# A streaming row maximum on one core: a tail recut into 29 loads, the clearing moved to GpSimd, and SyncE's implied waits dropped

## The chip, the cores and the metric

The kernel runs on one core of a Trainium2 chip. The metric is the device time of one execution in microseconds (us), as the median of several runs. A profiled execution also has a span, from the first to the last instruction of the program; in all profiles here the timed figure of the profiled run is 1.83 to 1.85 us above its span.

## The reference

```python
def setup_inputs():
    return {"x": np.random.randn(8192, 8192).astype(np.float32)}

def reference(x):
    return np.linalg.norm(x, ord=np.inf, axis=1)   # per row: the largest absolute value
```

268 MB are read once, and 8192 numbers are written.

## The kernel before

Rows lie on 128 partitions, 64 to a partition. The first 48 rows of each partition come in 24 bulk loads of two rows (16384 columns); VectorE reduces each in one instruction. The other 16 rows are the tail: seven tiles, each cut into some loads (`TAIL`), and a last tile whose cuts shrink to the end (`LAST`), so that little is left to reduce when the last byte has landed.

```python
TAIL = [
    [9728, 6656], [5632, 10752], [9600, 6784], [9344, 7040],
    [6784, 6528, 3072], [4736, 3072, 4224, 4352],
    [3968, 2432, 3072, 2944, 1792, 2176],
]
LAST = (      # (row of the pair, columns)
    [(0, w) for w in (2176, 2048, 1664, 1664)]
    + [(1, w) for w in (1536, 1280, 1152, 1024, 896, 896, 768)]
    + [(0, 640), (1, 640)]
)
...
nc.vector.memset(part[:], 0.0)
...
for j, (b, w) in enumerate(LAST):
    final = left[b] == 0
    ...
    nc.sync.dma_start(out=t[:, to : to + w], in_=...)
    if final:      # also reads the row's partial maxima, which lie just behind
        absmax(r_tail[:, r : r + 1], t[:, to : slot[b] + parts_of[b]])
    else:
        done = absmax(t[:, k : k + 1], t[:, to : to + w])
    ...
    if j == len(LAST) - 4:      # the bulk result's store waits for this reduction
        ins = nc.scalar.dma_start(out=out_b, in_=r_bulk[:])
        after(ins, done, ...)
nc.sync.dma_start(out=out_t, in_=r_tail[:])
```

The two final reductions of `LAST` wait for two things, a landing and VectorE's own counter (for the partial maxima). In the trace one of the two is a stand-alone wait, an instruction of its own in front of the reduction in VectorE's stream; here it is the wait for the landing (for the first of the two it ends at 622.25, and the reduction starts at 622.48).

## Time and profile before

| | kernel before, profiled run |
|---|---|
| time, median of the 3 first runs | 627.47 us |
| time of the profiled run itself | 627.57 us |
| span | 625.73 us |
| last bulk landing | 466.67 |
| last landing of all | 623.02 |
| end of VectorE's last reduction | 624.02 |
| store of the tail result issued, landed | 624.05, 625.47 |

Times inside a profile count from the start of the span. A landing is the issue of a load plus its time to landing. "Pitch" will mean the time from one VectorE start to the next when they run without a gap.

### The profile page before, as it was taken

What the parts mean: (1) busy time and instruction counts of PE and PEld (TensorE: products, weight loads), DVE (VectorE), ACT (ScalarE), POOL (GpSimd) and SP (SyncE); (2) the same over time, 40 slices, a digit from 0 to 9 for tenths busy, and PEclk for the clock granted to TensorE, in tenths of its full rate; (3) what the DMA queues carried; (4) which work ended last, traced back from release to release, by engine and by line L of the source; (5) the groups of instructions that cost most, each with busy time, mean ns of one, the idle gap of its engine ahead of it and who ended that gap; (6) DMA issues with size and microseconds to landing.
All of it is one profiled execution on the core that took longest, in us unless ns stands there. A gap on an engine that the chain in (4) does not pass through costs nothing.

```text
span 625.7 us, 205 instructions
## 1 busy us (share of the span) xinstructions
DVE 552.9 (88%) x67; POOL 0.2 (0%) x4
## 2 busy tenths in 40 slices
DVE  0588988889988889888898888988889999999998
POOL 0000000000000000000000000000000000000000
DMA  9999999999999999999999999999999999999997
GB/s 402 469 402 452 419 452 419 448 423 436 436 419 452 411 461 402 469 402 469 402 469 402 461 411 452 419 448 423 444 413 421 444 425 431 436 425 430 424 422 315
DMA packets 9282, 268.49 MB, mean 429 GB/s; under 512 B 1856, under 2 KB 1856, under 8 KB 3392
## 3 DMA queue, kind: packets, MB, share of 16 engines
q1 hardware_dynamic: 8496, 268.45, 99.5%
q10 hardware_dynamic: 784, 0.02, 0.1%
q14 instruction: 2, 0.02, 0.0%
HBM read 268.44 MB, written 0.03 MB: 429 GB/s over the span
## 4 chain that ended last, share of the span: by engine, by line
DMA 67%; DVE 31%; issue 1%; another core or an unknown queue 0%; DVEq 0%; SPq 0%
DMA t<-in_x_dram 67%; DVE r_bulk L140 24%; DVE part L140 6%; DVE t L140 2%; DVEq L230 0%; DVE r_tail L140 0%; SPq L159 0%
## 5 line engine op out<-in xcount | busy, mean ns | idle before, releaser
L140 DVE TENSOR_REDUCE r_bulk<-t 128x2 f32<-128x16384 f32 x24 | 413.3, 17220 | 69.7 <-DMA t<-in_x_dram 69.7
L140 DVE TENSOR_REDUCE part<-t 128x1 f32<-128x8192 f32 (+20 forms) x28 | 121.5, 4410 | 0.3 <-DMA t<-in_x_dram 0.3
L140 DVE TENSOR_REDUCE t<-t 128x1 f32<-128x1664 f32 (+8 forms) x11 | 16.7, 1576 | 0.2 <-DMA t<-in_x_dram 0.2
L140 DVE TENSOR_REDUCE r_tail<-t 128x1 f32<-128x644 f32 (+1 forms) x2 | 1.5, 814 | 0.0
L137 DVE MEMSET part<- 128x56 f32 x1 | 0.1, 105 | 0.9 <-PEq L219 0.9
L140 DVE TENSOR_REDUCE r_tail<-part 128x14 f32<-128x56 f32 x1 | 0.2, 201 | 0.0
L219 POOL MEMSET const-bfloat16-1.0<- 128x1 bf16 x1 | 0.1, 101 | 0.0
L219 POOL MEMSET const-uint8-127<- 128x1 uint8 x1 | 0.1, 101 | 0.0
L219 POOL MEMSET const-float32-0.0<- 128x1 f32 x1 | 0.1, 98 | 0.2 <-issue 0.2
L219 POOL MEMSET const-float32-1.0<- 128x1 f32 x1 | 0.1, 98 | 0.0
## 6 DMA issues: line engine op xcount, KB each, us to landing
t<-in_x_dram SPq DMA_DIRECT2D x2, 3392.0 KB, 37.2
t<-in_x_dram SPq DMA_DIRECT2D x1, 5376.0 KB, 40.5
t<-in_x_dram SPq DMA_DIRECT2D x1, 4864.0 KB, 32.9
t<-in_x_dram SPq DMA_DIRECT2D x1, 4800.0 KB, 32.9
t<-in_x_dram SPq DMA_DIRECT2D x1, 4672.0 KB, 34.7
t<-in_x_dram SPq DMA_DIRECT2D x3, 1536.0 KB, 36.9
t<-in_x_dram SPq DMA_DIRECT2D x1, 3520.0 KB, 42.7
t<-in_x_dram SPq DMA_DIRECT2D x1, 3328.0 KB, 40.4
```

Of the source, the lines that this page charges most:

```text
L137: nc.vector.memset(part[:], 0.0)
L140: return nc.vector.reduce_max(out=o, in_=i, axis=X, apply_absolute_value=True)
L219: nc = _bacc.Bacc("TRN2", target_bir_lowering=False, num_devices=1)
```

## The change

Its intent: fewer loads and fewer reductions in the tail (29 and 36 instead of 34 and 42), coarser cuts at the end, one instruction less on VectorE, and no waits on SyncE that another wait implies.

```diff
 TAIL = [
+    [6272, 10112],
+    [10112, 6272],
     [9728, 6656],
-    [5632, 10752],
-    [9600, 6784],
     [9344, 7040],
-    [6784, 6528, 3072],
-    [4736, 3072, 4224, 4352],
-    [3968, 2432, 3072, 2944, 1792, 2176],
+    [6144, 6784, 3456],
+    [6144, 5504, 4736],
+    [4352, 3840, 2816, 2944, 2432],
 ]
 LAST = (
-    [(0, w) for w in (2176, 2048, 1664, 1664)]
-    + [(1, w) for w in (1536, 1280, 1152, 1024, 896, 896, 768)]
-    + [(0, 640), (1, 640)]
+    [(0, w) for w in (2432, 2432, 2176)]
+    + [(1, w) for w in (1920, 1664, 1152, 1408, 1152)]
+    + [(0, 1152), (1, 896)]
 )
+def drop_implied_waits(nc):
+    ...   # of a load's waits, drop each that VectorE's instruction, waited for as well, has itself waited for
-    nc.vector.memset(part[:], 0.0)
+    nc.gpsimd.memset(part[:], 0.0)
...
+    nc.at_finalize(drop_implied_waits)
```

More of the change, by code (lines that the diff above doesn't have):

```diff
@@ L2 @@
+import copy
 import logging
@@ L96, in finish_on_pool @@
     end.instructions = [i for i in insts if i.name not in moved] + [wait, clear]
+def drop_implied_waits(nc):
+    sp, dve = mybir.EngineType.SP, mybir.EngineType.DVE
+    body = nc.main_func.blocks[-2]
+    insts = list(body.instructions)
+    counter, seen, upto = None, {}, []
+    for i in insts:
+        if i.engine != dve or i.sync_info is None:
+            continue
+        for s in i.sync_info.on_wait:
+            assert s.sync_type == "semaphore" and s.wait_mode == "sem-ge-imm"
+            seen[s.id] = max(seen.get(s.id, 0), s.wait_value)
+        for s in i.sync_info.on_update:
+            assert s.update_mode in ("sem-inc", "sem-add-imm")
+            assert counter in (None, s.id)
+            counter = s.id
+            upto += [dict(seen)] * s.update_value
+    for n, i in enumerate(insts):
+        if i.engine != sp or type(i).__name__ != "InstDMACopy":
+            continue
+        waits = i.sync_info.on_wait
+        at = [s.wait_value for s in waits if s.id == counter]
+        if len(waits) > 1 and at:
+            known = upto[max(at) - 1]
+            keep = [
+                s
+                for s in waits
+                if s.id == counter or s.wait_value > known.get(s.id, 0)
+            ]
+            insts[n] = copy.replace(
+                i,
+                sync_info=mybir.SyncInfo(
+                    on_wait=keep, on_update=list(i.sync_info.on_update)
+                ),
+            )
+    body.instructions = insts
 @with_exitstack
```

## The prediction

> **What bounds the kernel now.** I read the page first, then the DMA view, the busy times by stretch, the chain of work, the groups by form and the timeline of the last microseconds. The page:
>
> ```profile
> DMA  9999999999999999999999999999999999999997
> DMA packets 9282, 268.49 MB, mean 429 GB/s; under 512 B 1856, under 2 KB 1856, under 8 KB 3392
> q1 hardware_dynamic: 8496, 268.45, 99.5%
> L140 DVE TENSOR_REDUCE r_bulk<-t 128x2 f32<-128x16384 f32 x24 | 413.3, 17220 | 69.7 <-DMA t<-in_x_dram 69.7
> ```
>
> The load queue keeps the 16 DMA engines busy in all 40 slices; VectorE waits for loads in the bulk. The stretches (us, VectorE busy and instructions, GpSimd, clock, DMA share, GB/s) say where the rate is lower:
>
> ```profile
> 41.00:466.60 425.60, 378.84 (x22) 0.00 (x0) 1.00 1.00 433
> 466.60:600.00 133.40, 132.98 (x27) 0.00 (x0) 1.00 1.00 430
> 600.00:622.00 22.00, 21.77 (x15) 0.00 (x0) 1.00 1.00 416
> ```
>
> The DMA share stays 1.00 while the rate falls from 433 to 416 GB/s as loads shrink: a load costs something beyond its bytes. VectorE is busy 99% of the tail too, so both engines matter there. The chain (start, duration, what) dates the last bulk landing at 466.67 and shows the end:
>
> ```profile
> 425.94 40.74 DMA t<-in_x_dram
> 466.67 0.02 issue
> ...
> 590.91 21.42 DMA t<-in_x_dram
> 612.33 0.02 issue
> 612.35 9.89 DVE t L140 x8
> 622.25 0.23 issue
> 622.48 0.59 DVE r_tail L140
> ```
>
> From 612.35 the end is held by eight back-to-back reductions, not by a load. The timeline, rows from two answers of it, gives VectorE's rhythm and the last microseconds:
>
> ```profile
> 483.83 51.82 DVE L140 TENSOR_REDUCE part<-t 128x1 f32<-128x8192 f32 x9
> ...
> 621.73 0.41 ACTq L200 DMA_DIRECT2D out_dram<-r_bulk  x1
> 622.48 1.55 DVE L140 TENSOR_REDUCE r_tail<-t 128x1 f32<-128x644 f32 x2
> 624.05 0.35 SPq L202 DMA_DIRECT2D out_dram<-r_tail  x1
> ```
>
> Last, one row of the groups by form, and two of the DMA view of short stretches (the last load; the bulk result's store):
>
> ```profile
> L140 DVE TENSOR_REDUCE r_tail<-t 128x1 f32<-128x647 f32 x1 | 0.8, 815 | 0.0
> ```
>
> ```profile
> t<-in_x_dram SPq DMA_DIRECT2D x1, 320.0 KB, 8.8
> ```
>
> ```profile
> q10 hardware_dynamic: 784, 0.02, 7.5%
> ```
>
> The last load is issued at 614.18 and lands 8.84 later, at 623.02. Its reduction runs until 622.48 + 1.55 = 624.02, the store is issued at 624.05, and the span ends at 625.73: 1.68 us of store and closing barrier, which I take as fixed. The timed 627.47 is 1.74 above the span.
>
> [...]from 466.67 to 623.02 are 156.35 us; eight tiles of 16384 columns (512 B each over 128 partitions) take 154.20 us at 435.2 GB/s; the other 2.15 us over 34 loads are 0.063 us a load.[...] the nine reductions from 483.83 hold 49152 columns, 51.20 us at 0.96 GHz, so 0.62 us is left over 9, or 0.06 each after taking off the last one's overlap[...]. A single duration is longer than its pitch, columns / 0.96 GHz + 142 ns (647: 815).
>
> **The change part by part.**
>
> *Fewer loads.* Tail and last tile go from 21 + 13 = 34 loads to 19 + 10 = 29. Five times 0.063 is 0.32 us of DMA time, on the path of the last landing: 623.02 becomes about 622.70.
>
> *Fewer reductions.* VectorE's pieces go from 28 + 1 + 11 + 2 = 42 to 25 + 1 + 8 + 2 = 36. Six pitches' fixed parts are 0.36 us, but only useful if no new waiting comes in between, since the columns stay the same. I stepped through both tails with two rules: landings follow at columns x 1.1765 ns + 0.063 us; a reduction starts at the later of its landing + 0.03 and the last start + pitch. Before, the idle time sums to 0.83 us; after, to 1.28, as 6144, 4352 and 2432 columns are coarser to wait for. That takes 0.45 and more than eats the 0.36.
>
> *A wider end.* The last loads are 1408, 1152, 1152 and 896 where they were 896, 768, 640 and 640. Backwards from 622.70, an 896 load takes 1.117 us and a 1152 load 1.418, so the landings are 618.75, 620.17, 621.58, 622.70. The 1408 reduction starts at 618.78; pitch 1.527 puts the next at 620.31; pitch 1.260 would allow 621.57, its landing says 621.61; pitch 1.264 (1155 columns with the three partial maxima) puts the last at 622.88, 0.18 after its landing. It reads 901 elements: 0.939 + 0.142 = 1.080 us, where the 647 took 0.815. End: 623.96 against a measured 624.02. But the same stepping on the kernel before ends at 623.86, 0.16 short of the trace (the pipe's last loads do not land on a smooth line); if that error stays, the new end is 624.12. So the sum is between -0.06 and +0.10; I take +0.02.
>
> *The clearing on GpSimd.* VectorE's 0.1 us clearing lies at 0.87, long before the first landing at 21.97; nothing is gained. GpSimd's own runs after the opening barrier, equally hidden. It adds one semaphore to the closing waits. Built, these are five pairs where four were, and four of them fit before the store's landing: 0 to 0.05 us.
>
> *Implied waits.* SyncE's waits on a load that VectorE has consumed already end with the VectorE wait. Bulk loads are issued 40 us before they land and the queue never runs dry, so 0.
>
> *Smaller partial tile.* 42 values instead of 56 save [...]0.015 us, in the middle.
>
> *The bulk result's store.* It is still tied to the fourth reduction from the end, but that one now ends 3.6 us before the end of VectorE instead of 2.3. It took 7.5% of 5 us on each engine, 0.375 us. Before, it began after the last load's bytes. After, it is issued about 620.4 and its packets meet the last two loads.[...] With 0.18 us slack before the last reduction that is 0 to +0.2; I take +0.03.
>
> Sum: +0.02 + 0.01 + 0.03 = +0.06, so 627.5 us.
>
> **Rivals.** (1) *Landings alone set the end.* If VectorE really reaches the last load without a backlog, it ends at 622.70 + 0.03 + 1.08 = 623.81: -0.21, so 627.26. For it: six fewer reductions. Against: the chain shows eight reductions in a row without a gap. (2) *The store takes a full turn among the last loads.* The last landing moves to 623.07, VectorE ends at 624.18: +0.16, and with the 0.16 of the stepping +0.3, so 627.8. For it: its earlier issue.[...] (3) *The waits matter*, each costing SyncE time that holds back loads. It would show as DMA share under 1.00 in the bulk; that reads 1.00, so I give it almost nothing. (4) *Per-load cost is more than 0.063* where packets are small, since 416 GB/s rules at the end: 5 x 0.1 = 0.5 us off the landing, but the wider last reduction still stands, so 627.1 at best.
>
> **Range and chances.** The rivals span 627.1 to 627.8; another chip or day may add 0.1. I give 627.05 to 627.9. Faster by over 2% would need 614.9 us, under the 616.8 that the bytes alone take at 435.2 GB/s: 0.003. Slower by 2% needs 12.5 us of new stall in a queue that is 40 us ahead: 0.007. Within 2%: 0.99.
>
> **What would show each step right or wrong.** Last landing near 622.7; end of VectorE near 624.0; last reduction 1.08 us and starting about 0.2 after its landing; 433 GB/s unchanged in the bulk; store of the bulk result issued near 620.4 to 620.6, its packets among the last loads. Wrong would be: a last landing later than 623.0 (the store or the loads' cost), a gap before the last reduction (rival 1), a DMA share under 1 in the tail, or a bulk that moves at all.

Passages that no trace or run of this case shows are cut from it, and the cuts are marked. The numbers that stay can be read from the profile of the kernel before. A straight line through the tail's 34 steps from one landing to the next, against their columns, gives 1.1766 ns a column and 0.063 us a load; with 512 bytes a column that is 435.2 GB/s. (Without the one step that took 0.44 us longer, see below, it gives 1.1795 ns and 0.040 us, so the split hangs on that load.) No load of this profile took less than 1.1767 ns a column, which is what the 616.8 us for all bytes rests on. The 0.96 GHz stands for VectorE's columns: of the gapless reductions one of 8192 columns starts 8.593 us before the next and one of 896 columns 0.993 us, which is 1.042 ns a column, or 0.96 columns a ns, and 0.06 us fixed. The 0.015 us of the smaller partial tile is 14 columns at that rate. The 0.1 us for another chip or day was a guess; the kernel before's medians lie between 627.47 and 627.74 us in all rounds.

The forecast's sum came to +0.06 us: 0.02 for the loads, reductions and wider end, 0.01 for the clearing and the partial tile, 0.03 for the bulk result's store. Of the last term the estimate inside the bracket is cut (0.06 us, from how the store's packets and the loads' would share the DMA engines). What remains of it is the bracket, 0 to 0.2 us: the store's measured 0.375 us (the "full turn" of rival 2) less the 0.18 us of slack. The 0.03 is the pick from it; without it the sum is +0.03, and 627.47 still becomes 627.5.

## The result

The changed kernel took 627.82 us (median of 6 runs, 627.73 to 628.22), the kernel before 627.53 us in the same rounds (6 runs, 627.43 to 627.70). A ratio is always the mean time of one kernel's runs over the mean of the other's in the same rounds, so it is not quite the ratio of the medians: here 1.0006, with a 95% interval of 0.9993 to 1.0019. By the 2% rule it is the same, and the interval cannot tell it from no change. The median is 0.32 us above the predicted 627.5, of which 0.06 is the kernel before having moved from 627.47 to 627.53.

Times of this size must be read inside the profile. The same three stretches of the changed kernel:

```profile
41.00:466.60 425.60, 378.84 (x22) 0.00 (x0) 1.00 1.00 432
466.60:600.00 133.40, 132.16 (x24) 0.00 (x0) 1.00 1.00 431
600.00:622.00 22.00, 21.96 (x12) 0.00 (x0) 1.00 1.01 421
```

The bulk moves at the same rate, and the last stretch is faster: 421 GB/s against 416. The loads did gain. The chain of work that ended last:

```profile
606.26 2.69 DVE t L180
608.95 0.10 DVE r_tail L180
...
609.07 12.92 DVE t L180 x7
622.00 0.32 issue
622.31 0.68 DVE r_tail L180
```

The piece from 609.07 is VectorE without a gap, as before. Then come 0.32 us under "issue", time in which the engine waited for nothing that the profile shows. The timeline of the end:

```profile
619.12 2.87 DVE L180 TENSOR_REDUCE t<-t 128x1 f32<-128x1408 f32 x2
620.76 0.42 ACTq L240 DMA_DIRECT2D out_dram<-r_bulk  x1
622.31 2.35 DVE L180 TENSOR_REDUCE r_tail<-t 128x1 f32<-128x1155 f32 x2 [0.33 <-DVE t L180]
624.70 0.35 SPq L242 DMA_DIRECT2D out_dram<-r_tail  x1
```

And from the groups by form and the DMA view, the last reduction and the two last loads (issued at 606.18 and 611.65):

```profile
L180 DVE TENSOR_REDUCE r_tail<-t 128x1 f32<-128x901 f32 x1 | 1.1, 1082 | 0.0
```

```profile
t<-in_x_dram SPq DMA_DIRECT2D x1, 576.0 KB, 15.6
```

```profile
t<-in_x_dram SPq DMA_DIRECT2D x1, 448.0 KB, 11.3
```

The last load but one landed at 621.81, the last at 622.95. The reduction in front (1152 columns) started at 620.64, so its pitch of 1.26 us would have let the 1155 reduction start at 621.90. It started at 622.31, 0.41 us late by pitch and 0.50 after its data. The 0.33 in the bracket is the same hole counted from the end of the reduction in front, 621.98. The bracket names a VectorE instruction because VectorE's counter rose last before it; but the counter's value that the 1155 reduction waits for belongs to the third partial maximum of its row, whose reduction ended at 614.1. So the wait for the counter is not the cause.

One more line of the DMA view, for 622.9 to 623.4:

```profile
q14 instruction: 1, 0.01, 4.4%
```

This is one packet of 8192 bytes of kind instruction, as the profile names it, on queue q14, at 622.98, 0.67 us after the late start. The kernel before has such packets at 591.92 and 609.98, among the loads.

### The profile page after: what moved, and what is told of

Read it like the earlier page. It is cut to its first block, busy times and chain, and to the rows that moved or that the text cites. A ratio compares the mean times of both kernels' runs of the same rounds, so it can differ in the third digit from the quotient of the medians.

```text
span 626.4 us, 166 instructions
## 1 busy us (share of the span) xinstructions
DVE 552.5 (88%) x60; POOL 0.3 (0%) x5
## 4 chain that ended last, share of the span: by engine, by line
DMA 58%; DVE 40%; issue 2%; another core or an unknown queue 0%; DVEq 0%
DMA t<-in_x_dram 58%; DVE r_bulk L180 23%; DVE part L180 14%; DVE t L180 2%; DVEq L271 0%; DVE r_tail L180 0%
## 5 line engine op out<-in xcount | busy, mean ns | idle before, releaser
L180 DVE TENSOR_REDUCE part<-t 128x1 f32<-128x8192 f32 (+15 forms) x25 | 121.3, 4923 | 0.7 <-DMA t<-in_x_dram 0.7
L180 DVE TENSOR_REDUCE t<-t 128x1 f32<-128x2432 f32 (+5 forms) x8 | 15.6, 2011 | 0.0
L180 DVE TENSOR_REDUCE r_tail<-t 128x1 f32<-128x1155 f32 (+1 forms) x2 | 2.4, 1218 | 0.3 <-DVE t L180 0.3
```

What stands on the lines that cost most here:

```text
L180: return nc.vector.reduce_max(out=o, in_=i, axis=X, apply_absolute_value=True)
```

## Reading all profiles on one scale

The last bulk landing moved between 466.60 and 467.40 from profile to profile, with no order that I found: the kernel before had 466.67 and 466.73, the changed kernel 467.16 and 467.01. The change leaves the bulk's loads and reductions as they are and drops only waits of SyncE there; the DMA share is 1.00 in both. The traces put the differences in the first landing (21.75 to 22.2 us) and in single loads early in the bulk: in again the eighth load landed 19.66 us after the seventh, in keep_waits the tenth 19.85 after the ninth, where before has 19.35 and 19.32. After the thirteenth load all fourteen profiles agree within 0.03 us a load. The rounds also ran on different chips (2, 4 and 15). So the table counts from the last bulk landing, but for the packets, which are in the span's own time. "Late" is the 1155 reduction's start beyond pitch and landing; "packet" is when the last packet of kind instruction comes; "last landing" and "VectorE's end" are us after the last bulk landing; "step" is the largest time beyond columns x 1.1765 ns (435.2 GB/s, the line of the kernel before) that any load of the last tile took.

| kernel | last landing | VectorE's end | late | packet at | step | time, median | before, same rounds |
|---|---|---|---|---|---|---|---|
| before | 156.34 | 157.35 | none | 609.98 | 0.44 | 627.47 | |
| before_again | 156.42 | 157.43 | none | 609.61 | 0.45 | 627.68 | 627.57 |
| changed | 155.79 | 157.51 | 0.41 | 622.98 | 0.10 | 627.82 | 627.53 |
| again (unaltered) | 155.78 | 157.50 | 0.43 | 622.82 | 0.10 | 627.86 | 627.62 |
| store_late | 155.72 | 157.48 | 0.41 | 622.64 | 0.10 | 627.89 | 627.62 |
| keep_waits | 155.79 | 157.50 | 0.42 | 623.51 | 0.10 | 627.90 | 627.58 |
| pad_end | 155.77 | 157.48 | 0.41 | 622.55 | 0.10 | 627.97 (1 run) | 627.57 |
| pad_front | 155.99 | 157.41 | none | 610.03 | 0.36 | 627.61 (1 run) | 627.57 |
| dve_clear | 155.91 | 157.27 | none | 609.73 | 0.25 | 627.65 | 627.58 |
| swap | 155.79 | 157.08 | none | 621.56 | 0.11 | 627.46 | 627.57 |
| swap_again | 155.76 | 157.06 | none | 621.63 | 0.10 | 627.63 | 627.74 |
| old_last | 156.09 | 157.10 | (no such reduction) | 609.58 | 0.35 | 627.74 | 627.62 |
| swap_old_last | 156.20 | 157.18 | (no such reduction) | 607.51 | 0.42 | 627.61 | 627.74 |
| old_cuts | 156.21 | 157.22 | (no such reduction) | 609.28 | 0.31 | 627.70 | 627.62 |

The tail repeats within 0.1 us: 157.35 and 157.43 for the kernel before, 157.51 and 157.50 for the changed one. So the change costs about 0.11 us in the tail (157.50 less the mean of the two, 157.39). The timed medians show more (0.29 and 0.24). The excess of 0.18 and 0.13 is little more than the 0.11 by which an identical copy of the kernel before came out above it (before_again, ratio 1.0001, 0.9989 to 1.0014). But noise should fall on both sides, and it doesn't: in all ten comparisons with five or six runs of an altered kernel, the time lies above what the tail says (VectorE's end less 157.39), by 0.08 us (swap_old_last) to 0.41 (old_last); for the copy it is 0.07. This is so with the old cuts, with the clearing on VectorE and with the waits kept, so no single part of the change accounts for it. It stays open.

## The experiments

Twelve kernels ran, all correct. Each edit is against the changed kernel unless it says otherwise.

**again**: no edit.

> The changed kernel, unaltered. Its first profile is 0.65 us longer than that of before: 0.48 us were lost before the last bulk landing (467.16 against 466.67), the tail's loads took 155.79 us instead of 156.35, and the last reduction but one (1155 columns) began at 622.31, 0.41 us after VectorE's usual pitch allowed it (621.90) and 0.50 after its data landed (621.81). Theory A, the late start belongs to the kernel: it shows again, 0.3 to 0.5 us, and the paired ratio is 1.0003 to 1.0008. Theory B, both losses are one run's accident: last bulk landing near 466.7, the 1155 reduction at most 0.1 us late, ratio 0.9998 to 1.0002.

Measured: 627.86 us against 627.62, ratio 1.0004 (0.9992 to 1.0017). The last bulk landing was 467.01. The late start is there again, 0.43 us. So Theory A holds for the late start; the loss in the bulk is not decided by this run, but the other profiles spread over it.

**store_late**: the bulk result's store tied to one reduction later.

```diff
-        if j == len(LAST) - 4:
+        if j == len(LAST) - 3:
```

> The bulk result's store tied to the next reduction (third from the end instead of fourth), so that its packets start after the last load's bytes. Rival 2 of the prediction (the store among the last loads delays the end): last landing minus last bulk landing falls from 155.79 to about 155.5, and the time by 0 to 0.2 us. If the issue of that store or its packets is also what holds the 1155 reduction back by 0.41 us, that delay goes too, and the time falls by 0.4 us or more against the changed kernel. If neither: same time within 0.1 us, delay still there.

Its timeline, where the store's issue and the late reduction stand:

```profile
621.68 0.41 ACTq L240 DMA_DIRECT2D out_dram<-r_bulk  x1
621.97 2.35 DVE L180 TENSOR_REDUCE r_tail<-t 128x1 f32<-128x1155 f32 x2 [0.33 <-DVE t L180]
```

The store is issued over a microsecond later, counted from the last bulk landing, and the last landing comes 0.07 us sooner (155.72), so rival 2 costs next to nothing. The hole in front of the 1155 reduction stays: 627.89 against 627.62, ratio 1.0005 (0.9993 to 1.0018). The store is not its cause.

**old_last**: the old `LAST`, all else changed.

> All of the change but the old cuts of the last tile (13 loads, ending in 640 and 640). If the wider end is what costs, this is at or below before: ratio 0.9994 to 1.0001, VectorE's last reduction 0.815 us, no late start. If the new cuts of the seven tail tiles, the clearing on GpSimd or the dropped waits cost, it stays at 1.0004 or more.

Measured: 157.10 to VectorE's end, 0.29 less than the kernel before and 0.41 less than the changed one; 627.74 us against 627.62, ratio 1.0003 (0.9990 to 1.0017), which is above what I expected of the ratio while the tail is below. No late start. Against old_cuts (157.22, below) the new cuts of the seven tiles are worth 0.12, and the new last tile takes that back and more.

**old_cuts**: `TAIL` and `LAST` as before; only the clearing and the dropped waits.

> Only the clearing on GpSimd and the dropped waits; all cuts as before. My step said 0 to 0.05 us: ratio 0.9999 to 1.0001. If the closing waits (five instead of four) or the start cost, the span after the last VectorE instruction grows from 1.71 us (624.02 to 625.73), or the first landing moves from 21.97, and the ratio is 1.0002 or more.

Measured: from VectorE's end to the end of the span 1.74 us against 1.71, so five closing waits cost at most 0.03. First landing 21.93. The tail is 157.22, a little shorter than before; 627.70 us against 627.62, ratio 1.0002 (0.9990 to 1.0015), 0.0001 over what I expected. In the tail these two parts cost nothing by themselves.

**swap**: each of VectorE's instructions with two waits gets them the other way round.

```diff
+def wait_for_data_last(nc):      # run with the other rewrites at the end of the build
+    ...
+        if len(waits) > 1:       # VectorE instructions only
+            waits.sort(key=lambda s: s.id not in counter, reverse=True)
+            ...                  # so the stand-alone wait is for VectorE's own counter
```

> The changed kernel, with the two waits of VectorE's three double-waiting reductions exchanged: the stand-alone wait is for VectorE's own counter (long reached), and the wait for the landing goes into the reduction itself[...]. In three profiles the 1155 reduction started 0.41, 0.43 and 0.41 us later than pitch and landing allowed, right after such a stand-alone wait for the landing. Theory S[...]: the delay is gone, VectorE's end minus the last bulk landing falls from 157.50 to about 157.1. Theory D (the delay is in the data or in the engine, e.g. the 1155 columns or the partial maxima it reads): unchanged, 157.5.

What the run tests is whether the delay goes with the stand-alone wait for the landing.

```profile
618.76 2.87 DVE L206 TENSOR_REDUCE t<-t 128x1 f32<-128x1408 f32 x2
620.40 0.41 ACTq L266 DMA_DIRECT2D out_dram<-r_bulk  x1
621.55 2.34 DVE L206 TENSOR_REDUCE r_tail<-t 128x1 f32<-128x1155 f32 x2
```

The bracket is gone: the 1155 reduction starts at its pitch (620.29 + 1.26), and VectorE ends 157.08 after the last bulk landing, 0.42 sooner than in the changed kernel. 627.46 us against 627.57, ratio 0.9997 (0.9983 to 1.0010). This is theory S's forecast, and theory D falls: same columns, same partial maxima, same data, and no delay. Note that the two waits are the same two; only which of them stands alone has changed.

**pad_front**: four tiny VectorE instructions at the very start.

```diff
     nc.gpsimd.memset(part[:], 0.0)
+    pad = outp.tile([P, 1], F32)
+    for _ in range(4):
+        nc.vector.memset(pad[:], 0.0)
```

> The changed kernel with four tiny VectorE clearings of a spare value at the very start, which moves all later VectorE instructions four places on in their stream. Theory F ([...]the delay is at a place in the stream counted from its start; the profile has one 8192-byte transfer of kind instruction at 622.98, 622.82 and 622.64, 0.67 us after the late start each time): the delay leaves the 1155 reduction, and that transfer comes at another instruction, 4 places earlier in the program. If the delay belongs to the stand-alone wait in front alone: still 0.41 us at 1155.

Two rows of the timeline, one of them from the time of the packet:

```profile
611.49 2.42 DVE L183 TENSOR_REDUCE t<-t 128x1 f32<-128x2176 f32 x1 [0.23 <-DMA t<-in_x_dram]
...
621.72 2.34 DVE L183 TENSOR_REDUCE r_tail<-t 128x1 f32<-128x1155 f32 x2
```

More VectorE instructions, and the late start is gone, although the stand-alone wait for the landing is still in front of the 1155 reduction. The packet comes at 610.03 now, and a load pays: the 2176 columns landed 0.36 us beyond their bytes, 0.02 in the changed kernel. But the packet now comes while the second reduction of the last tile runs, where it came after the last but one: some seven instructions of the program earlier, not four as I expected.

**pad_end**: four tiny VectorE copies after the last reduction.

```diff
     nc.sync.dma_start(out=out_t, in_=r_tail[:])
+    for _ in range(4):
+        nc.vector.tensor_copy(out=pad[:], in_=r_tail[:, n_tail - 1 :])
```

> The changed kernel with four tiny VectorE copies after the last reduction, which nothing waits for but the closing barrier; the places counted from the start stay, those counted from the end move by four. If the place counts from the start (theory F as above) the delay of 0.41 us at the 1155 reduction stays[...].

Cut is the rival to it: a place counted from the end of the stream, with which the delay would go or move.

```profile
621.87 2.35 DVE L181 TENSOR_REDUCE r_tail<-t 128x1 f32<-128x1155 f32 x2 [0.32 <-DVE t L181]
```

The delay stays, 0.41 us, with the packet at 622.55. What lies in front of it in the stream matters, and these instructions behind it don't.

**before_again**: the kernel before, no edit.

> The kernel before, unaltered, for a second profile. It tells how far its parts repeat: last bulk landing 466.67 (the five profiles of changed kernels have 466.60 to 467.16), from there to VectorE's end 157.35. If the second repeats within 0.1 while the first moves by some tenths, then the bulk is noise and the tail is what the change can be judged by: +0.15 us. If the bulk stays at 466.6 to 466.7, the changed kernels' later bulk would need a cause.

Measured: tail 157.43, last bulk landing 466.73, 627.68 us (627.53 to 628.31) against 627.57 of the same code. It is the measure of what a median of five runs can tell: about 0.1 us, no better.

**dve_clear**: the clearing back on VectorE.

```diff
-    nc.gpsimd.memset(part[:], 0.0)
+    nc.vector.memset(part[:], 0.0)
```

> The changed kernel with the clearing of the partial maxima back on VectorE, which puts every later VectorE instruction one place further on in its stream. [...]the late one is now the stand-alone wait in front of the 1155 reduction, which has to wait for the landing anyway: the delay is hidden, VectorE's end minus the last bulk landing falls from 157.50 to between 157.1 and 157.25, with the instruction transfer still near the end. If the delay stays at 1155, the place does not count from the start after all. That VectorE's clearing costs time by itself would show as a first reduction later than the first landing.

"The late one" is the instruction at theory F's place, counted from the start of the stream, which was assumed here to come 0.4 us late.

```profile
621.68 2.34 DVE L180 TENSOR_REDUCE r_tail<-t 128x1 f32<-128x1155 f32 x2
```

One instruction more, and the delay is gone: 157.27. That is 0.02 over my bracket and the packet isn't where I expected it: it comes at 609.73 and not near the end, and the 2176 load pays 0.25 us. 627.65 against 627.58, ratio 1.0002 (0.9990 to 1.0015).

**keep_waits**: SyncE's implied waits kept.

```diff
-    nc.at_finalize(drop_implied_waits)
```

> The changed kernel with SyncE's implied waits kept, 92 instructions on SyncE instead of 63. The kernel before had two transfers of kind instruction in the tail (near 592 and 610), each kernel with dropped waits has one. [...]the one near 592 was SyncE's; here it is back, somewhere between 585 and 605, and the load under way lands about 0.3 us later, as the 1664 load did in before (0.44 us beyond its bytes instead of 0.03): last landing minus last bulk landing 155.9 to 156.2 instead of 155.79. If dropping the waits does nothing for the loads: one transfer, 155.79.

Measured: the second packet is back, at 597.57, so that one comes with SyncE's longer stream (92 instructions instead of 63). But no load pays for it: the last landing is 155.79, as without it, and VectorE's end 157.50. My 155.9 to 156.2 was wrong. 627.90 against 627.58, ratio 1.0003 (0.9989 to 1.0016).

**swap_again** and **swap_old_last**: the exchanged waits once more, and with the old `LAST`.

> The exchanged waits once more, unaltered, to see whether the gain repeats: VectorE's end minus the last bulk landing 157.08 within 0.05, the 1155 reduction at its pitch, time 627.4 to 627.6, a tenth or so below the kernel before of the same rounds. An identical copy of the kernel before came out 0.11 us above it, so less than that in the time alone decides nothing.

> The exchanged waits with the old last tile (13 loads, ending in 640 and 640). With the late instruction out of the way, is the new last tile worth anything? The old one had 157.10 without exchanged waits, its last reductions at VectorE's pitch, so exchanging should change nothing: 157.05 to 157.15, equal to the new last tile's 157.08. If the exchange also moves the instruction transfer out of the loads (it came at 609.58 there and the 1664 load under way took 0.35 us beyond its bytes), it is 156.8 or less, and the old last tile is the better one.

swap_again repeats: 157.06, start at pitch, 627.63 us (0.03 over what I expected) against 627.74, ratio 0.9997 (0.9985 to 1.0010). swap_old_last has 157.18 and 627.61 us, ratio 0.9997 (0.9984 to 1.0011): not better than the new last tile, and 0.03 over what I expected of its tail. It shows something else. The exchange moved the packet from 609.58 to 607.51, and the load that pays moved with it: in old_last the second 1664 load took 0.35 us beyond its bytes and the first 0.02; here the first took 0.42 and the second 0.02.

## Why the prediction was right or wrong

*Fewer loads.* Right in direction, mis-sized, and one cause was missing: the step that failed here is "0.063 us a load". I charged 0.063 us a load, from 2.15 us over 34 loads of the kernel before. But 0.44 of the 2.15 is one load of 1664 columns. These are the rows of the kernel before on which that stands, the packet and the one reduction of the tail's end that had to wait for a landing:

```profile
q14 instruction: 1, 0.01, 1.9%
```

```profile
610.25 1.88 DVE L140 TENSOR_REDUCE t<-t 128x1 f32<-128x1664 f32 x1
...
612.35 1.89 DVE L140 TENSOR_REDUCE t<-t 128x1 f32<-128x1664 f32 x1 [0.23 <-DMA t<-in_x_dram]
```

All seven profiles with the packet between 607 and 611 have such a step, 0.25 to 0.45 us, in the load then under way or next in line; all seven with it at 621 or later have none above 0.11. And the step followed the packet in swap_old_last. So in these profiles a load near this packet lands 0.25 to 0.45 us late when it comes among the loads. The packet took 0.31 us (1.9% of sixteen engines' 1 us), about the size of the step; how it holds the load back is not shown. SyncE's packet, near 592 and at 597.57, took as long and shows no step, and I can't say why. The change moved the packet behind the loads. Of the 0.59 us that the last landing gained (156.38 to 155.79), this is about 0.42, which leaves 0.17 for the five loads, 0.03 each and not 0.063.

*Fewer reductions.* Six pitches less, against new idle time. The idle time of the tail's reductions, summed over the page's groups, went from 0.5 us (0.3 and 0.2) to 1.0 (0.7 and 0.3); of the latter 0.33 is the hole before the 1155 reduction. Without the hole it grew by 0.2, not by the 0.45 of my stepping.

*A wider end.* The last reduction took 1.082 us where I had 1.080. The main step of the prediction that failed is this: "pitch 1.260 would allow 621.57, its landing says 621.61", with which the 1155 reduction was to start. In the profile pitch allowed 621.90 and the landing said 621.81, and it started at 622.31. That 0.41 us was in none of the parts, nor in the rivals: all of them asked when data lands and when the engine is free, and none had room for a reduction that starts later than both. swap shows what was lost: without the hole, VectorE ends at 157.08 and not at 157.50, where the stepping had 157.29 (623.96 less 466.67). The stepping was too pessimistic by 0.21, mostly because the last landing came 0.24 sooner than it assumed, and the hole more than took that back.

*Why the instruction was late.* Shown: the delay is not the data, the columns, the store or the waits as such; it goes when VectorE's stand-alone wait in front no longer is the one for the landing (twice), it goes when one or four instructions are put in front in the stream (two kernels), and it stays when four are put behind. Nor does a stand-alone wait cost 0.4 us as such. The trace has it as an instruction of its own: in the five profiles with the delay the 1155 reduction starts 0.45 to 0.47 us after this instruction ends (621.86, then 622.31 in the changed kernel), in dve_clear 0.13 and in pad_front 0.18 after, both at VectorE's pitch. In four of the five profiles with the delay the packet of kind instruction follows the late start by 0.66 to 0.68 us, and in the fifth (keep_waits) by 0.97.

Not shown: what holds the 1155 reduction back. The packet of kind instruction comes with the delay, but no trace shows an instruction that waits for it. What stays open too is at which place in the stream the packet comes. One instruction in front moved the packet by some seven instructions of the program and four by as many, and the old `LAST`, with three reductions more, moved it though all in front was equal; no count from the start or from the end that I tried fits all fourteen profiles. In six of the seven with the packet among the loads it comes while the second reduction of the last tile runs, whether 52 or 56 VectorE instructions had started by then.

*The clearing on GpSimd.* I gave it 0 to 0.05 us, and its own cost is that: 1.72 us from VectorE's end to the end of the span, 1.71 before. But dve_clear shows that taking this one instruction from VectorE's stream is part of what made the 1155 reduction late: 157.50 with the clearing on GpSimd, 157.27 with it on VectorE (one profile). So the move cost 0.23 us through the place of other instructions, not through its own work.

*Implied waits.* Right: keep_waits has the same tail to 0.01 us. They shortened SyncE's stream and removed one instruction packet, at no gain.

*Smaller partial tile.* 188 ns instead of 201 for its reduction; right, and too small to see.

*The bulk result's store.* Right: moving it out of the last loads brought the last landing forward by 0.07 us, far under its full 0.375, and VectorE's end by 0.03. It did meet the last loads: in the changed kernel, from 621.74 to the end of the loads' last packet at 622.55, 714 of its 784 packets started and took 48.9% of the DMA engines' time, the loads' 25.9%. I had it issued near 620.4; it was 620.76 on a span whose bulk ended 0.48 later.

*Rivals.* Rival 1 (no backlog on VectorE) did not happen: 609.07 to 622.00 is one unbroken piece. Rival 2 put 627.8 on the store; the time came out there by luck, not by its mechanism. Rival 3 is not borne out by keep_waits: the same tail, and 0.32 us above the kernel before where the changed one was 0.29 and 0.24 above. Rival 4 guessed a per-load cost above 0.063; it is below.

*What of the +0.29 us stays open.* 0.11 is shown in the tail. The rest, 0.18 in these rounds and 0.13 in those of again, is little more than the identical copy shows against itself, but it has the same sign in every comparison (see the table's section); in the profiles it lies before the last bulk landing. I found no cause for it and claim none.

*The base.* The prediction's "1.74 above the span" sets the median of three runs (627.47) against the span of a run that took 627.57; within that run it is 1.84. Only differences were used, so nothing rests on it.

## What to carry to other kernels

When an instruction has two waits, let the stand-alone one be the wait that is over long before, and leave the wait that ends last in the instruction itself: here that was worth 0.42 us at the end of a chain, and it gave the shortest tail of all (157.06 and 157.08; in time 0.11 us below the kernel before in both sets of rounds, which alone would not be clear of noise). It is no gain everywhere: with the old `LAST`, where nothing was late, the exchange gave 157.18 against 157.10. At the scale of tenths of a microsecond, adding or removing an instruction that has no cost of its own can make another one late at the end (157.27 with the clearing on VectorE, 157.50 without), so judge such a change by the profile of the part it touches, from a fixed event, and not by the whole time.
